# The prompt's second FFN product taken into the latents' seven products, and FFN stores issued by GpSimd

## The chip, the cores and the metric

The kernel runs on one core of a Trainium2 chip. The metric is the time of one execution in microseconds of the device; the kernel before was timed three times, with a median of 2180.29 us (2177.92 to 2182.85). The engines are TensorE (PE, matmuls), VectorE (DVE), ScalarE (ACT), GpSimd (POOL) and SyncE (SP); DMAs are issued from the instruction queues of SP, ACT or POOL and carried by 16 DMA engines.

## The reference, cut to what matters

One layer of a hybrid diffusion backbone on 1024 latent tokens and 256 prompt tokens, 1024 channels, all in float32. The token mixers come first and are not touched. What matters here is the end of the layer, which both kinds of token go through with the same weights, but with their own modulation (`sh2`, `sc2`, `g2`):

```python
    h = rms_norm(x, norm_ffn_w) * (1.0 + sc2) + sh2
    x = x + g2 * (jnp.square(jax.nn.relu(h @ w_ff1)) @ w_ff2)
...
y_prompt = rms_norm(xp, final_norm_w)
y_sample = rms_norm(xs, final_norm_w)
```

`w_ff1` is 1024 x 4096 and `w_ff2` 4096 x 1024. The other three outputs (keys, values and scan states of the prompt) are written long before.

## The kernel before, in words

**Splitting.** Every float32 product is made of three matmuls on two halves of each operand: `split` writes the high half on ACT (L270) and the rest on DVE (L271), and PE adds high x high, high x low and low x high (L299 to L301 in the first product, L1309 to L1311 and L1434 to L1436 in the latents' products, L1565 to L1567 in the prompt's second).

**The prompt's first product** (loop at L1255) goes over 16 blocks `i` of 256 of the 4096 hidden channels, each in two half-blocks of 128. A half-block loads its share of `w_ff1` (tile `wraw`, two buffers), splits it (`wsp`), and runs 24 matmuls of 128x256, the weights standing and the 256 prompt tokens moving. ACT takes relu and square into `ap` (L1232 to L1234, two buffers), and one store a block puts both halves into a DRAM tensor `AP_[i]`. Beside it, DVE and ACT prepare the latents' activations: their second norm, the sums that the seven products need (`sums1`, L1241 to L1251) and their splits (`form`).

**The latents' first product** (loop at L1313) computes, for each of the 16 blocks, a 2x2 block product in seven products instead of eight (Winograd's form of Strassen's scheme: sums of weight quarters against sums of activation quarters). Three PSUM banks X, Y, Z are used by turns: product 1 into X, which ACT copies to `s1` (L1318); product 2 into Y, to which DVE adds `s1` as `u2` (L1321); product 3 adds to X; and so on. Each block gives the four quarters after relu and square and the three sums that the second product needs. These seven forms go to DRAM with seven stores a block (L1348 to L1355), each of 512 columns, issued, as all stores of `store` (L101), from ACT's queue.

**The latents' second product** runs its seven products one after the other, in the order P1, P2, P6, P7, P4, P5, P3 (`chain2`, L1422). A product has 16 steps, one for each 256 hidden channels; a step loads one form of the activations (`ar`) and a weight quarter (`wr`, or `a11c` in P1, kept for later) three steps ahead, splits both (`ah`, `wh`) and runs 12 matmuls of 128x512 into four banks. Between the products DVE adds a product's banks to the residual (`gadd`, L1449, and the sums `u2`, `u3`). Within P5 the first half of the latents is normed and stored (`final`, L1459).

**The prompt's second product** follows as a stage of its own: 32 steps, each of which loads 128 rows of `w_ff2` again, splits them (`w2s`), and runs 12 matmuls of 128x512 with the prompt's activations standing (`mm_p`, L1559). The second half of the latents is normed beside it, and `final_p` (L1569) norms and stores the prompt at the end.

Each engine runs its instructions in the order of its own list, which a scheduler fixes when the kernel is built; an instruction that waits holds up all behind it on that engine. Tiles come from pools with a fixed number of buffers: a new tile in a used buffer waits for the old one's last readers, stores included. The pool `ev` of the latents' first product is opened where the pool `pw` of the prompt's was closed, so its tiles lie on the same memory.

Of the kernel before, what the change touches and what calls it, by code (L numbers as in the profile page):

```python
# [9 lines left out]
F32 = mybir.dt.float32  # L10
# [5 lines left out]
P = 128  # L16
D = 1024
# [27 lines left out]
def build(ctx, tc, I, O, C):  # L45
# [55 lines left out]
    def store(out, in_):  # L101
        s_.dma_start(out=f32(out), in_=f32(in_))
# [1125 lines left out]
    AP_ = [DR((P, 2, 256), "AP%d" % i) for i in range(NP)]  # L1228
    AF_ = {f: [DR((P, 512), "AF%s_%d" % (f, i)) for i in range(NP)] for f in FORMS}
# [26 lines left out]
    for i in range(NP):  # L1256
        r = raw1(i)
        for half in range(2):
# [5 lines left out]
            if half == 0:  # L1264
                e = pw.tile([P, 2, 256], F32, tag="ap", name="ap", bufs=2)
            relu2(e[:, half], po[:, 0:256])
            if half:
                store(AP_[i], e)
# [44 lines left out]
    for i in range(NP):  # L1313
# [34 lines left out]
        store(AF_["B11"][i], a11)  # L1348
        store(AF_["B22"][i], a22)
        store(AF_["T1"][i], t1)  # L1350
        store(AF_["T3"][i], t3)
        store(AF_["B21"][i], a21)
        store(AF_["T2"][i], t2)
        v.tensor_tensor(a12, a21, t2, op=ALU.subtract)
        store(AF_["T4"][i], a12)  # L1355
# [5 lines left out]
    sc2 = pool("s2c")  # L1361
    ac = pool("a11c", "right")
    a11c, s2c = {}, {}
# [14 lines left out]

    def load_a11(i):
        a11c[i] = quarter((0, 0), i, ac.tile([P, 512], F32, tag="a11_%d" % i, name="a11c"))  # L1380
        return a11c[i]

    def make_s2(i, x, y):
        s = wsum(x, y, ALU.add)
        s2c[i] = sc2.tile([P, 512], F32, tag="s2_%d" % i, name="s2c")
        v.tensor_tensor(s2c[i], s, a11c[i], op=ALU.subtract)
# [12 lines left out]
    def load_step(n):  # L1399
# [4 lines left out]
        ar = st.tile([P, 512], F32, tag="ar", name="ar", bufs=4)  # L1404
        dma(ar, AF_[STEP[name][0]][i])
# [8 lines left out]
        if n == 54:  # L1414
            load_fw()

    def rsp(tag, src):
        hi, lo = [st.tile([P, 512], F32R, tag=tag, name=tag, bufs=8) for _ in range(2)]
        split(hi, lo, src)
        return hi, lo  # L1420

    def chain2(name, banks, first, at=None):  # L1422
        for i in range(NP):
# [3 lines left out]
            ah, al = rsp("ah", ar)  # L1427
            wh, wl = rsp("wh", STEP[name][2](i, *ws_))
# [3 lines left out]
            for m in range(4):  # L1432
                c = slice(m * P, (m + 1) * P)
                pe.matmul(banks[m], wh[:, c], ah, start=first and i == 0, stop=False, **more)  # L1434
                pe.matmul(banks[m], wh[:, c], al, start=False, stop=False, **more)  # L1435
                pe.matmul(banks[m], wl[:, c], ah, start=False, stop=i == NP - 1, **more)  # L1436
# [7 lines left out]
    def cs(name):  # L1444
        return xo.tile([P, 512], F32, tag="cs", name=name, bufs=12)
# [14 lines left out]
    def final(t, b):  # L1460
# [3 lines left out]
        for i in range(2):  # L1464
# [3 lines left out]
            jk = xo.tile([P, 512], F32, tag="jk", name="jk", bufs=1)  # L1468
            s_.activation(jk, pt, AF.Square, accum_out=ss[:, i:i + 1])
# [3 lines left out]
        for i, pt in enumerate(pts):  # L1473
            y = xo.tile([P, 512], F32, tag="y", name="y", bufs=3)
# [3 lines left out]
    def four():  # L1478
        return [PS(x) for x in "ggss"]

    def load_p(kb):

        if kb >= NK:
            return
        early = kb < NQ1
        p, k = (q1, "e") if early else (q2, "l")
        if kb % 2 == 0 or kb == NQ1:
            aps[0] = p.tile([P, 2, 256], F32, tag="apr" + k, name="apr", bufs=2 if early else 4)
            dma(aps[0], AP_[kb // 2])
        wr = p.tile([P, D], F32, tag="w2p" + k, name="w2p", bufs=1 if early else 4)  # L1490
        dma(wr, W2[kb * P:(kb + 1) * P, :])
        got_p[kb] = aps[0][:, kb % 2], wr

    def prep_p(kb):
        early = kb < NQ1
        p, k = (q1, "e") if early else (q2, "l")
        ar, wr = got_p.pop(kb)
        hl = p.tile([P, 2, 256], F32R, tag="aph" + k, name="aph", bufs=NQ1 if early else 6)
# [154 lines left out]
```

## Time and profile before

| what | value |
|---|---|
| median of 3 runs | 2180.29 us |
| profiled execution | 2176.4 us, its span 2174.6 us, mean granted clock 0.988 |
| PE busy | 2085.2 us (96% of the span) |
| DVE, ACT, POOL busy | 1410.5, 981.1, 445.2 us |
| prompt's first product | 1341.0 to 1432.7 us |
| latents' first product | 1432.7 to 1742.3 us |
| latents' second product | 1749.9 to 2072.8 us |
| prompt's second product and last norms | 2072.8 to 2174.6 us |

Times in the trace are counted from the span's start. A row of a group gives the line, the engine, what it writes and reads with sizes, the count, busy time and mean, and the idle time of the engine just ahead of it with what ended it. A row of a timeline gives start, duration and, in brackets, idle time before. Rows with a q at the engine's name (ACTq, SPq) are the issue of a DMA in that engine's queue; POOL's own issues stand under POOL.

### The profile page before, as it was taken

The page shows a single profiled execution, that of the slowest core. Times are in us where ns is not written, and L with a number is a line of the kernel's source. Part 1 is how long each engine was busy: PE and PEld are TensorE (multiplying, and loading weights), DVE is VectorE, ACT ScalarE, POOL GpSimd, SP SyncE. Part 2 cuts the span into 40 slices and gives each one's busy share as a digit, 9 for nine tenths or more (in the row PEclk, how much of TensorE's full clock was granted, in tenths as well). Part 3 has the DMA queues.
Part 4 walks back from the last instruction along what each step waited for, and adds up shares of the span by engine and source line. Part 5 has one row for each costly group of instructions (what it writes and reads, how often), then busy time and mean ns, then how long its engine had stood idle before and what let it go on. Part 6 is the DMA issues. An engine that isn't in the chain of part 4 may idle for free. (4 is left out here: it accounts for less than half of the span.)

```text
span 2174.6 us, 34820 instructions
## 1 busy us (share of the span) xinstructions
PE 2085.2 (96%) x12907; PEld 1795.3 (83%) x12907; DVE 1410.5 (65%) x2642; ACT 981.1 (45%) x1994; POOL 445.2 (20%) x416
## 2 busy tenths in 40 slices
PE   6899999999999998999999999999999989999998
PEld 4788889988899877787888888988888878887786
DVE  3784776777776867768353536856666577666765
ACT  4754555555555422222220426745444444444453
POOL 1471233333233445445112000000000000000000
PEclk9999999999999999999999999999999999999999
DMA  9364222132122434445534433754444397567673
GB/s 287 106 201 141 69 73 70 53 117 78 53 68 74 148 117 147 142 144 160 191 127 131 128 117 107 225 173 138 157 137 154 134 318 264 188 196 254 220 273 138
DMA packets 266186, 327.14 MB, mean 150 GB/s; under 512 B 18952, under 2 KB 172112, under 8 KB 266016
## 3 DMA queue, kind: packets, MB, share of 16 engines
q1 hardware_dynamic: 244384, 285.80, 41.1%
q10 hardware_dynamic: 21312, 38.81, 4.8%
q8 instruction: 101, 1.65, 0.3%
q0 software_dynamic: 320, 0.31, 0.1%
q14 instruction: 69, 0.57, 0.1%
HBM read 240.44 MB, written 84.41 MB: 149 GB/s over the span
## 5 line engine op out<-in xcount | busy, mean ns | idle before, releaser
L299 PE MATMUL ps_g<-hs,wsp 128*128 128x512 f32 (+1 forms) x960 | 360.1, 375 | 2.4 <-DVE modc L190 2.4
L301 PE MATMUL ps_g<-hs,wsp 128*128 128x512 f32 (+1 forms) x960 | 343.6, 358 | 0.0
L300 PE MATMUL ps_g<-hs,wsp 128*128 128x512 f32 (+1 forms) x960 | 343.1, 357 | 0.0
L677 POOL TENSOR_SCALAR pexp<-pexp,rs 128x512 f32<-128x512 f32 (+1 forms) x104 | 169.1, 1632 | 367.7 <-ACT pTh L702 179.3
L270 ACT ACTIVATE wsp<-wraw 128x1024 fp32r<-128x1024 f32 x118 | 117.9, 1001 | 245.6 <-PE ps_g L300 115.1
L271 DVE TENSOR_TENSOR wsp<-wraw,wsp 128x1024 fp32r<-128x1024 f32 x118 | 141.9, 1204 | 121.0 <-ACT wsp L270 120.6
L299 PEld LDWEIGHTS ps_g<-hs,wsp 128*128 128x128 f32 x960 | 183.9, 192 | 27.2 <-issue 4.8
L301 PEld LDWEIGHTS ps_g<-hs,wsp 128*128 128x128 f32 x960 | 182.8, 190 | 27.5
L300 PEld LDWEIGHTS ps_g<-hs,wsp 128*128 128x128 f32 x960 | 183.9, 192 | 19.7
L702 ACT ACTIVATE pTh<-ps_t 128x512 fp32r<-128x512 f32 x200 | 119.0, 601 | 130.4 <-PE ps_t L699 127.4
L164 POOL TENSOR_TENSOR frst<-ms,mexp 128x1 f32<-128x1 f32 x10 | 7.2, 719 | 813.4 <-DVE ms L163 803.7
L659 DVE TENSOR_REDUCE mx<-ps_s 128x1 f32<-128x512 f32 (+1 forms) x208 | 136.7, 662 | 50.4 <-PE ps_s L658 49.8
L669 ACT ACTIVATE pexp<-ps_s,ngm 128x512 f32<-128x512 f32 (+1 forms) x208 | 137.3, 669 | 44.9 <-DVE ngm L663 43.3
L270 ACT ACTIVATE ah<-ar 128x512 fp32r<-128x512 f32 x112 | 70.7, 631 | 163.5 <-PE ps_s L1435 141.5
L703 DVE TENSOR_TENSOR pTl<-ps_t,pTh 128x512 fp32r<-128x512 f32 x200 | 135.8, 679 | 13.1 <-ACT pTh L702 12.7
L658 PE MATMUL ps_s<-Kl,Ql 128*128 128x512 f32 (+1 forms) x416 | 128.6, 413 | 1.5 <-ACT pexp L669 1.5
L699 PE MATMUL ps_t<-ident,pexp 128*128 128x128 f32 x800 | 120.7, 272 | 2.4 <-DVE pexp L677 1.3
L315 PE MATMUL ps_g<-wsp,hs 128*128 128x256 f32 x400 | 117.0, 292 | 0.0
L316 PE MATMUL ps_g<-wsp,hs 128*128 128x256 f32 x400 | 113.6, 284 | 2.8 <-DVE wsp L271 2.8
L317 PE MATMUL ps_g<-wsp,hs 128*128 128x256 f32 x400 | 113.6, 284 | 0.0
L271 DVE TENSOR_TENSOR ah<-ar,ah 128x512 fp32r<-128x512 f32 x112 | 77.1, 688 | 54.8 <-ACT ah L270 53.4
L715 PE MATMUL ps_g<-pTl,Vl 128*128 128x256 f32 x400 | 105.6, 286 | 4.5 <-DVE pTl L703 4.5
(362 smaller groups left out, 5449.8 us busy)
## 6 DMA issues: line engine op xcount, KB each, us to landing
wraw<-in_w_ff SPq DMA_DIRECT2D x32, 1024.0 KB, 5.7
wr<-in_w_ff SPq DMA_DIRECT2D x128, 256.0 KB, 4.0
wraw<-in_w_in SPq DMA_DIRECT2D x19, 1024.0 KB, 6.0
wraw<-in_w_ada SPq DMA_DIRECT2D x16, 1024.0 KB, 5.4
ar<-AFT SPq DMA_DIRECT2D x64, 256.0 KB, 2.7
w2p<-in_w_ff SPq DMA_DIRECT2D x32, 512.0 KB, 4.7
AFB<-a ACTq DMA_DIRECT2D x48, 256.0 KB, 2.2
AFT<-t ACTq DMA_DIRECT2D x48, 256.0 KB, 2.1
```

The lines of the kernel that those rows point to most:

```text
L270: s_.activation(hi, raw, AF.Copy)
L271: v.tensor_tensor(lo, raw, f32(hi), op=ALU.subtract)
L299: pe.matmul(out, hi[:, k, :], mh, start=(first and k == 0), stop=False)
L300: pe.matmul(out, hi[:, k, :], ml, start=False, stop=False)
L301: pe.matmul(out, lo[:, k, :], mh, start=False, stop=(last and k == kcs - 1))
L658: pe.matmul(pq[:, 0:n], self.qh[:, q0:q0 + P], K[self.g][var][self.kts[i]], start=(var == 0), stop=(var == 1))
L659: v.tensor_reduce(self.mx[j][:, i:i + 1], pq[:, 0:n], axis=AX.X, op=ALU.max)
L669: s_.activation(e[:, 0:n], self.ps.pop((j, i))[:, 0:n], AF.Exp, bias=self.mx[j], accum_out=self.sm[j][:, i:i + 1])
L677: NORM[(i + j) % len(NORM)].tensor_scalar(x, x, self.rs[j], None, op0=ALU.mult)
L699: pe.transpose(pt[:, a, j * P:(j + 1) * P], self.Ps[j][i][:, b * P:(b + 1) * P], ident)
L702: s_.activation(hi, pt, AF.Copy)
L703: v.tensor_tensor(lo, pt, f32(hi), op=ALU.subtract)
```

## The change

All stores of `store` are issued by GpSimd. The stores of the prompt's and the latents' activations now go to one DRAM tensor a block, `AFD[i]`, of seven forms by 640 columns: 512 of the latents, 128 of the prompt. For that, the prompt's 256 hidden channels of a block and its two halves of 128 tokens are taken as a 2x2 block matrix too, and DVE makes the four sums of its quarters as four subtractions of 128x128 into a tile `apf` with one buffer; three stores a block replace one.

In the second product a step loads 640 columns and splits them together; its weights, split for the latents, serve the prompt as well: three further matmuls of 128x512 (`mm_p`), into a fifth bank. P3's prompt matmuls are put off to the end: its split weights and activations are kept, in buffers that `a11c` and the sums `s2c` no longer need, and run there as 48 matmuls, alternating with the norms of the latents' second half. The stage of the prompt's second product goes, with its loads and splits. `final_p(0)` moves into P5. The output buffers `y` go from 3 to 2, the buffers `cs` for sums and copies of products from 12 to 8; they now also serve the squares' unused output and the prompt's sums.

```diff
     def store(out, in_):
-        s_.dma_start(out=f32(out), in_=f32(in_))
+        g_.dma_start(out=f32(out), in_=f32(in_))
...
-    AP_ = [DR((P, 2, 256), "AP%d" % i) for i in range(NP)]
-    AF_ = {f: [DR((P, 512), "AF%s_%d" % (f, i)) for i in range(NP)] for f in FORMS}
+    AFD = [DR((P, 7, 640), "AF%d" % i) for i in range(NP)]
...
             if half:
-                store(AP_[i], e)
+                f = pw.tile([P, 4, P], F32, tag="apf", name="apf", bufs=1)
+                b11, b12, b21, b22 = e[:, 0, 0], e[:, 0, 1], e[:, 1, 0], e[:, 1, 1]
+                v.tensor_tensor(f[:, 0], b12, b11, op=ALU.subtract)
+                v.tensor_tensor(f[:, 1], b22, b12, op=ALU.subtract)
+                v.tensor_tensor(f[:, 2], b22, f[:, 0], op=ALU.subtract)
+                v.tensor_tensor(f[:, 3], b21, f[:, 2], op=ALU.subtract)
+                store(AFD[i][:, 0:2, 512:640], e[:, :, 0])
+                store(AFD[i][:, 2, 512:640], b22)
+                store(AFD[i][:, 3:7, 512:640], f)
...
-        ar = st.tile([P, 512], F32, tag="ar", name="ar", bufs=4)
-        dma(ar, AF_[STEP[name][0]][i])
+        ar = st.tile([P, 640], F32, tag="ar", name="ar", bufs=4)
+        dma(ar, AFD[i][:, FI[STEP[name][0]]])
...
+    def mm_p(bank, i, a, w, first, last):
+
+        (ph, pl), (wh, wl) = a, w
+        more = dict(skip_group_check=not first)
+        pe.matmul(bank, ph, wh, start=first and i == 0, stop=False, **more)
+        pe.matmul(bank, pl, wh, start=False, stop=False, **more)
+        pe.matmul(bank, ph, wl, start=False, stop=i == NP - 1, **more)
...
+            if name != "P3":
+                mm_p(banks[4], i, (ah[:, 512:640], al[:, 512:640]), (wh, wl), first, False)
...
     def cs(name):
-        return xo.tile([P, 512], F32, tag="cs", name=name, bufs=12)
+        return xo.tile([P, 512], F32, tag="cs", name=name, bufs=8)
...
-            y = xo.tile([P, 512], F32, tag="y", name="y", bufs=3)
+            y = xo.tile([P, 512], F32, tag="y", name="y", bufs=2)
...
+    chain2("P2", X, False, {2: make_g2b})
...
+    chain2("P6", Y, True)
+    for m in range(4):
+        gadd(1, m, plus(Y[m], sk[m]))
+    padd(1, 0, plus(Y[4], sk[4]))
+    chain2("P7", Y, False)
...
+    at = {3 * b + 2: lambda b=b: final(0, b) for b in range(4)}
+    at[14] = lambda: final_p(0)
+    chain2("P5", Z, True, at)
+    for m in range(4):
+        gadd(1, 4 + m, Z[m])
+    padd(1, 1, Z[4])
+    chain2("P3", Z, False)
+    for m in range(4):
+        gadd(1, m, Z[m])
+    for i in range(NP):
+        mm_p(Z[4], i, p3f[i], p3w[i], False, True)
+        if i % 4 == 3:
+            final(1, i // 4)
+    padd(1, 0, Z[4])
+    final_p(1)
```

Three places show how the engines' lists change. In the rows, the names in brackets are what an instruction waits for: an engine, or a counter of landed DMAs (DMAHW for those that SP or ACT issued, DMASW for those of POOL).

First, DVE in the prompt's first product. In before, `wsp` are the low halves of the weights of half-blocks 18 and following (the first row is half-block 19), `form` and `xa` belong to the latents' sums:

```order
L271 TENSOR_TENSOR form<-xa,form 128x512 [waits DVE_49]
L1251 TENSOR_TENSOR xa<-xa 128x512 [waits DVE_49]
L271 TENSOR_TENSOR wsp<-wraw,wsp 128x1024 [waits PE_49,Activation_49]
L271 TENSOR_TENSOR form<-xa,form 128x512 [waits Activation_49]
L271 TENSOR_TENSOR wsp<-wraw,wsp 128x1024 [waits DMAHW0_49,PE_49,Activation_49]
L271 TENSOR_TENSOR form<-xa,form 128x512 [waits Activation_49]
L271 TENSOR_TENSOR wsp<-wraw,wsp 128x1024 [waits PE_49,Activation_49]
```

After the change, the same place on DVE; `apf` 4 is the first group of four, `apf` 5 the second:

```order
L1252 TENSOR_TENSOR xa<-xa 128x512 [waits DVE_49]
L271 TENSOR_TENSOR form<-xa,form 128x512 [waits Activation_49] x2
L1271 TENSOR_TENSOR apf<-ap 128x128 [waits DMASW7_49]
L1272 TENSOR_TENSOR apf<-ap 128x128
L1273 TENSOR_TENSOR apf<-ap,apf 128x128 [waits DVE_49]
L1274 TENSOR_TENSOR apf<-ap,apf 128x128 [waits DVE_49]
L1271 TENSOR_TENSOR apf<-ap 128x128 [waits DMASW2_49,DVE_49]
L1272 TENSOR_TENSOR apf<-ap 128x128
L271 TENSOR_TENSOR wsp<-wraw,wsp 128x1024 [waits PE_49,Activation_49]
L1273 TENSOR_TENSOR apf<-ap,apf 128x128 [waits DVE_49]
L1274 TENSOR_TENSOR apf<-ap,apf 128x128 [waits DVE_49]
L271 TENSOR_TENSOR wsp<-wraw,wsp 128x1024 [waits DMAHW0_49,PE_49,Activation_49]
```

Both last `form` rows now stand ahead of the weights of half-block 19, and so do `apf` 4 and, with its wait for the store of `apf` 4 (DMASW2), the first half of `apf` 5.

Second, the passage from the prompt's to the latents' first product. DVE before: the last split ahead of the latents' loop, and `u2` of the first block (`u`):

```order
L271 TENSOR_TENSOR wsp<-ws,wsp 128x1024 [waits PE_49,Activation_49]
L1292 TENSOR_TENSOR ws<-wraw,ws 128x512 [waits DVE_49]
L1321 TENSOR_TENSOR u_16765<-ps_s,s_16751 128x512 [waits PE_49,Activation_49]
L271 TENSOR_TENSOR wsp<-wraw,wsp 128x512 [waits PE_49,Activation_49]
L271 TENSOR_TENSOR wsp<-wraw,wsp 128x1024 [waits PE_49,Activation_49]
```

DVE after, from `apf` 13 on; the split and `apf` 12 stand just ahead of these rows:

```order
L1271 TENSOR_TENSOR apf<-ap 128x128 [waits DMASW2_49,DVE_49]
L1272 TENSOR_TENSOR apf<-ap 128x128
L1273 TENSOR_TENSOR apf<-ap,apf 128x128 [waits DVE_49]
L1274 TENSOR_TENSOR apf<-ap,apf 128x128 [waits DVE_49]
L1271 TENSOR_TENSOR apf<-ap 128x128 [waits DMASW5_49,DVE_49,Activation_49]
L1272 TENSOR_TENSOR apf<-ap 128x128 [waits Activation_49]
L1273 TENSOR_TENSOR apf<-ap,apf 128x128 [waits DVE_49]
L1274 TENSOR_TENSOR apf<-ap,apf 128x128 [waits DVE_49]
L1271 TENSOR_TENSOR apf<-ap 128x128 [waits DMASW0_49,DVE_49,Activation_49]
```

ACT after, at the same place; the last row is the copy `s1` of the first block, which before waited for PE alone:

```order
L270 ACTIVATE wsp<-ws 128x1024 [waits PE_49]
L1234 ACTIVATE ap<-ps_s 128x256 [waits DMASW6_49,DMASW5_49,DVE_49]
L1234 ACTIVATE ap<-ps_g 128x256
L1235 ACTIVATE ap<-ap 128x256 [waits Activation_49] x2
L1234 ACTIVATE ap<-ps_s 128x256 [waits DMASW1_49,DMASW0_49,DVE_49]
L1234 ACTIVATE ap<-ps_g 128x256 [waits PE_49]
L1235 ACTIVATE ap<-ap 128x256 [waits Activation_49] x2
L1327 ACTIVATE s_16751<-ps_g 128x512 [waits DMASW2_49,DMASW4_49,DMASW1_49,DMASW5_49,DMASW0_49,DMASW7_49,DVE_49,PE_49]
```

Four `apf` groups moved between the last split and `u2`, each behind the landing of the one before, and `s1` now waits for six counters, that of the last `apf` store (DMASW1) among them.

Third, ACT at the start of the latents' second product, before. The rows L102 are stores:

```order
L1234 ACTIVATE a_19030<-a_19030 128x512 [waits Activation_49]
L270 ACTIVATE ah<-ar 128x512 [waits DMAHW1_49]
L102 DMA AFT_15_15490<-t_19036 128x512 [waits DMAHW6_49,DVE_49]
L102 DMA AFB_15_15442<-a_19030 128x512 [waits DMAHW0_49,Activation_49]
L102 DMA AFT_15_15458<-t_19035 128x512 [waits DMAHW2_49,DVE_49]
L102 DMA AFT_15_15522<-u_18955 128x512 [waits DMAHW4_49,DVE_49]
L270 ACTIVATE wh<-a11c 128x512
```

And after:

```order
L1234 ACTIVATE a_19030<-a_19030 128x512 [waits DVE_49]
L1235 ACTIVATE a_19030<-a_19030 128x512 [waits Activation_49]
L270 ACTIVATE ah<-ar 128x640 [waits DMAHW6_49]
L270 ACTIVATE wh<-a11c 128x512 [waits DMAHW7_49]
L270 ACTIVATE ah<-ar 128x640 [waits DMAHW0_49]
```

The four stores ahead of the first split of weights are gone from ACT's list.

More of the change, by code (lines that the diff above doesn't have):

```diff
@@ L1556, in build, with five @@
[L1556 to L1567 removed]
+    def five():
+        return [PS(x) for x in "ggssg"]
```

211 lines of the change are left out of this document (80 added, 131 removed).

## The prediction

> **What bounds the kernel now.** I read first the busy times by stage, cut where the matmuls change line; the columns are the stretch, its length, then busy microseconds of PE, weight load, DVE, ACT and POOL, the granted clock, the DMA share and GB/s. In order: the prompt's first FFN product, the latents' first product, a gap, the latents' second product, the prompt's second product with the last norms.
>
> ```profile
> 1341.00:1432.70 91.70, 88.60 (x740) 87.25 (x739) 72.15 (x90) 71.56 (x130) 1.53 (x1) 1.00 0.69 217
> 1432.70:1742.30 309.60, 309.60 (x1346) 252.00 (x1344) 191.24 (x261) 146.22 (x222) 0.00 (x0) 1.00 0.42 142
> 1742.30:1749.90 7.60, 0.16 (x1) 0.00 (x0) 3.78 (x6) 2.42 (x5) 0.00 (x0) 0.69 0.76 261
> 1749.90:2072.80 322.90, 315.25 (x1376) 258.74 (x1377) 225.84 (x360) 139.10 (x248) 2.91 (x4) 0.98 0.72 240
> 2072.80:2165.30 92.50, 92.50 (x433) 77.02 (x431) 56.55 (x85) 46.54 (x80) 3.75 (x5) 1.00 0.62 213
> ```
>
> PE is busy in all of it, so matmuls left out pay in full and a stall on any engine that PE waits for costs in full. The waits of PE in the first of these stages name its only supplier that is late, the DVE half of the weight split:
>
> ```profile
> PE ps_g L301 <- DVE wsp L271: 1.8, 2, 1.1
> PE ps_s L301 <- DVE wsp L271: 1.3, 2, 0.9
> ```
>
> So that stage, which the change loads with DVE work, is already limited by DVE in places.
>
> **Gains, in the second product.** First the group of a product's matmuls by its two kinds of bank (total, mean ns, idle time before), then single matmuls (start, duration, idle time before in brackets).
>
> ```profile
> L1434 PE MATMUL ps_g<-ah,wh 128*128 128x512 f32 x224 | 89.0, 397 | 14.2 <-ACT wh L270 7.5 <-DVE xa L1449 6.7
> L1434 PE MATMUL ps_s<-ah,wh 128*128 128x512 f32 x224 | 88.5, 395 | 0.9 <-DVE u L1524 0.4 <-DVE xa L1449 0.3 <-DVE u L1529 0.2
> ```
>
> ```profile
> 2021.52 0.39 PE L1435 MATMUL ps_s<-ah,wh 128*128 128x512 f32 x1
> 2021.75 0.39 PE L1436 MATMUL ps_s<-ah,wh 128*128 128x512 f32 x1
> 2026.81 0.76 PE L1434 MATMUL ps_g<-ah,wh 128*128 128x512 f32 x1 [4.68 <-DVE xa L1449]
> ...
> 2032.01 0.39 PE L1434 MATMUL ps_g<-ah,wh 128*128 128x512 f32 x1
> ```
>
> A matmul of 512 columns follows the last by 0.227 us (2021.52 to 2021.75); after an idle 4.7 us, 12 of them take 2032.01 - 2026.81 = 5.2, 0.43 each: 5.2 - 12 x 0.227 = 2.4 us of lost clock for each long idle time.
> - Matmuls: the prompt's 384 become 7 x 48 = 336. 48 x 0.227 = **-10.9 us**. 288 run inside the steps (+65.4 us there), 48 at the end.
> - Start of the product: the next rows are ACT's queue and ACT.
>
> ```profile
> 1744.19 0.63 ACT L1234 ACTIVATE a<-a 128x512 f32<-128x512 f32 x1 [0.34 <-ACT a L1233]
> ...
> 1745.40 0.95 ACTq L102 DMA_DIRECT2D AFT<-t  x1
> 1748.88 0.33 ACTq L102 DMA_DIRECT2D AFT<-u  x1
> 1749.25 0.63 ACT L270 ACTIVATE wh<-a11c 128x512 fp32r<-128x512 f32 x1 [3.92 <-DMA AFT<-t]
> ```
>
> The first split of weights stood behind a store that waited for an earlier store. Without stores, ACT ends its last square at 1744.8, splits 640 and 512 columns (0.7 and 0.6), and PE starts near 1745.9 instead of 1749.9: **-4.0 us**.
> - Stalls between the seven products: 14.2 - 7.5 + 0.9 + 2.4 of clock = 10 us. A step lasts 15 x 0.227 = 3.40 us instead of 2.72 for 225.84/112 = 2.0 us of DVE, to which 128 more columns add some 0.13 us; this relief works for it, fewer shared buffers (12 to 8) that put DVE's sums of products between PE and its next weights work against it. I take **0** (bounds +5 and -10).
> - End: before, 101.8 us from the end of the last latent product (2072.8) to 2174.6, of which 384 x 0.227 = 87.1 matmuls: 14.7 of other work. After, the last 48 matmuls alternate with four norms, whose two PSUM banks and two output buffers free at the store's landing. One norm to its second output:
>
> ```profile
> 2162.76 0.17 DVE fss L1578
> 2163.82 0.76 DVE yo L1583
> 2164.61 2.12 DMA out_y_prompt<-yo
> ```
>
> ```profile
> L102 ACTq DMA_DIRECT2D out_y_prompt<-yo x4: 338/338/339, 2164.6 to 2171.5; - x4
> ```
>
> First 12 matmuls 2.7; transposes, squares and these steps about 4.5; three more norms at a period of about 3.9 (y at 2163.82, its store landed at 2166.73, then the next y) 11.7; the prompt's own last pair 3.6; last store to the end 2174.6 - 2171.5 = 3.1. Sum 25.6, of it 10.9 matmuls: 14.7, as before. The gate transposes that move into P2 add 1.8: **+1.8** (bounds 0 and +8).
> Sum: -10.9 - 4.0 + 0 + 1.8 = **-13.1 us** (bounds 0 and -25). W2 is no longer read twice and 32 splits go, but they ran under PE's 92.50: nothing. 64 stores become 160; POOL had no work in these stages.
>
> **Losses, in the first product.** Here the new work is `apf`: per block of 256 channels four DVE operations of 128x128 in one single buffer, whose store must have landed before the next block's first operation. This is the DVE queue around half-block 19 of 32 in before, and PE's start of it:
>
> ```profile
> 1393.98 1.21 DVE L271 TENSOR_TENSOR wsp<-wraw,wsp 128x1024 fp32r<-128x1024 f32 x1
> 1395.12 0.68 DVE L271 TENSOR_TENSOR form<-xa,form 128x512 fp32r<-128x512 f32 x1
> 1396.05 1.23 DVE L271 TENSOR_TENSOR wsp<-wraw,wsp 128x1024 fp32r<-128x1024 f32 x1 [0.25 <-ACT wsp L270]
> 1397.20 0.68 DVE L271 TENSOR_TENSOR form<-xa,form 128x512 fp32r<-128x512 f32 x1
> 1397.83 1.23 DVE L271 TENSOR_TENSOR wsp<-wraw,wsp 128x1024 fp32r<-128x1024 f32 x1
> 1403.42 2.36 DVE L271 TENSOR_TENSOR wsp<-wraw,wsp 128x1024 fp32r<-128x1024 f32 x2 [4.36 <-ACT wsp L270]
> ```
>
> ```profile
> 1396.06 0.28 PE L299 MATMUL ps_g<-h2p,wsp 128*128 128x256 f32 x1
> ```
>
> DVE has no gap up to 1399, and PE begins half 19 0.9 us after its weights (1393.98 + 1.2). In the new order these weights stand behind the two last form splits (2 x 0.6), `apf` 0 to 4 and two operations of `apf` 5, which wait for the store of `apf` 4. Prices, the first two of them a 128x128 operation and the landing of the old `AP` stores in this stage (min, median, max), then landings and POOL's issue elsewhere:
>
> ```profile
> L429 DVE TENSOR_TENSOR vst<-kve,vst 128x128 fp32r<-128x128 f32 x10 | 3.1, 335 | 0.9 <-ACT vst L428 0.9
> ```
>
> ```profile
> DMA to landing us min/median/max: 2.0/3.9/6.0
> ```
>
> ```profile
> AFT<-t ACTq DMA_DIRECT2D x48, 256.0 KB, 2.1
> mask<-const_masks POOLq DMA_DIRECT2D x2, 64.0 KB, 8.2
> rows<-in_b_ada POOLq DMA_DIRECT2D x1, 24.0 KB, 3.3
> ```
>
> ```profile
> 3.94 0.51 POOL L122 DMA_DIRECT2D rows<-in_hgrn_lb_logits  x1
> ```
>
> A 128x128 operation lasts 0.34 us there; 512 columns are followed after 0.63 (1397.20 to 1397.83), a quarter of which is 0.16. I take 0.25, in between, and 1.0 for the four. The turnaround t, from `apf`'s end to the next `apf`, is two semaphores (an estimate of 0.1 each), the landing, and POOL's issue, 0.2 us longer than ACT's 0.33. Bounds 2.1 (nearest store, quiet DMA) and 6.4 (AP's slowest), 8.2 for POOL's own at the program's start, when DMA was full. In this stage (DMA share 0.69) I take AP's 3.9 + 0.4 = 4.3; after it (0.42) between AFT's 2.1 + 0.4 and POOL's least 3.3 + 0.2: 3.1.
> - Half 19: 1.2 + 22 x 0.25 + 4.3 - 0.9 = **+10.1 us**, and **+2.4** of clock. From there a block's DVE loop is 1.0 + 4.3 = 5.3 us, two weight splits (2.3) lying in the wait, under PE's pitch of 91.7/16 = 5.7: no further loss unless t exceeds 4.7. Behind `apf` on ACT wait the squares of the block after next and with them its next splits; that loop is 4.8 us (1.4 squares, 1.0 split on ACT, 1.2 on DVE, 1.0 `apf`, 0.2), also covered. On POOL the next block's other two stores stand ahead of an `apf` store, issued by then.
> - The stage's end. Rows of ACT, then DVE:
>
> ```profile
> 1432.82 1.06 ACT L270 ACTIVATE wsp<-ws 128x1024 fp32r<-128x1024 f32 x1 [1.03 <-PE ps_g L300]
> 1433.79 0.36 ACT L1233 ACTIVATE ap<-ps_g 128x256 f32<-128x256 f32 x1
> 1435.73 0.60 ACT L1318 ACTIVATE s<-ps_g 128x512 f32<-128x512 f32 x1 [1.13 <-PE ps_g L1311]
> ```
>
> ```profile
> 1434.05 1.22 DVE L271 TENSOR_TENSOR wsp<-ws,wsp 128x1024 fp32r<-128x1024 f32 x1
> 1438.59 0.69 DVE L1321 TENSOR_TENSOR u<-ps_s,s 128x512 f32<-128x512 f32 x1 [2.72 <-PE ps_s L1311]
> ```
>
> PE leaves the stage at 1432.7 (call it 0). The split at 1434.05 waits for that end, so it is done at 2.4; in the new order `apf` 12, 13, 14 and 15 all stand behind it, each waiting for the one before to land. `apf` 12 with one sum: to 3.9. Then three times t + 1.0, then t until `apf` 15 has landed. Only then may the copy `s1` (L1318 before, 0.6) be written, since its tile lies where `apf` lay, and PE's third product of the latents, which adds to the bank that `s1` copies, stands behind it on PE. It was due at 24 x 0.23 = 5.5. Stall: 3.9 + 3.0 + 4t + 0.6 - 5.5 = 2.0 + 4t, at t = 3.1 **+14.4 us** (10.4 at 2.1, 27 at 6.4), and **+2.4** of clock. Nothing later gives it back: PE is busy 309.60 of the next 309.60.
> Sum of losses 10.1 + 14.4 + 4.8 = **+29.3 us**.
>
> The Trainium skill, page "SBUF — State Buffer", section "SBUF: two separate sides", speaks against stores on GpSimd: their descriptors are written by GpSimd, and a DVE copy in a two-port mode locks it out, so that a transfer of about 0.62 us took 3.1. No row here shows GpSimd issuing beside a busy DVE. By that rule each of the five turnarounds would be an estimated 2.5 us longer, and the sum 12 us higher.
>
> **Total.** -13.1 + 29.3 = +16.2 us on the profiled execution's 2176.4 (span 2174.6 and 1.8 around it): 2192.6. That execution lies 3.9 under the median 2180.3, so against the median the time is **2196.5**.
>
> **Rivals.**
> - The turnaround sets the stage's pace. If t is 6.4 in both places (AP's slowest), half 19 costs 12.2, six more blocks 6 x (7.4 - 5.7) = 10, the end 27.6, clock 4.8: +54.6 - 13.1, 2222. At t = 5: 10.8 + 2 + 22 + 4.8 - 13.1 = +26.5, 2207. For it: AP's range and POOL's 8.2; against: AP's median. By the Trainium skill's page it would be this case, 2209. Chance 0.22.
> - Half 19 isn't late: DVE has hidden room (shorter 128x128 operations, an early landing). Then 12.5 go and 2184 remains. Against: PE waited for DVE there already. Chance 0.12.
> - Not slower: the second product gains its full bound. With 3.40 us steps DVE is never late at the product boundaries (-10) and PE's start stays warm (-2.4): -25.5. It decides if all five boundaries show under 1 us of idle time. At my t that is 2184; with t = 2.6 in both places (losses 8.4 + 12.4 + 4.8) 2180.4, no change. Against: L1449's sums in DVE's queue remain. Chance 0.13.
>
> **How the numbers follow.** The forecast, both stalls paid and t near my values, has 0.53: 2187 to 2206. The range that leaves out 2 in 10 goes from 2179 (the third rival) to 2214 (t near 5.5). A run tells 0.2%, 4.4 us, from no change. Slower: forecast, first rival, a third of the second and third: 0.83. Within: most of those two, 0.12. Faster needs both bounds at once: 0.05.
>
> **What would show it.** Right: PE idle near 10 us in the prompt's first product with DVE `apf` behind a landing of its store, and 10 to 20 us after the latents' second product with ACT's `s1` behind that landing; the start of the second product idle under 4 us; under 30 us from P3's end. Wrong: PE without a gap there, `apf` to landing far from 3 to 4 us, or boundaries of the second product that cost over 15 us.

## The result, and the profile after

The changed kernel takes **2202.46 us** (median of 4 runs, 2200.76 to 2210.59) against 2180.65 for the kernel before on the same chip (4 runs, 2177.92 to 2182.85): a ratio of 1.0108, 95% interval 1.0081 to 1.0135, so slower by 0.8 to 1.35%. The prediction was 2196.5, with a range of 2179 to 2214.

The profiled execution is the longest of the four, 2210.59 (span 2208.5). Of the 34 us that lie between it and the profiled execution of before, 10.8 stand ahead of the prompt's first product, where nothing was changed (that product starts at 1346.3 in place of 1335.5). This is spread between runs: the median less the length of the stages from there on is 1340.3 for the changed kernel and 1341.6 for the kernel before. So stages are compared. The prompt's first product and the second product count from their own first matmul, the other stages from the end of the last matmul ahead of them. First the changed kernel; the columns are the stretch, its length, busy microseconds of PE, weight load, DVE, ACT and POOL, the granted clock, the DMA share and GB/s:

```profile
1346.30:1453.40 107.10, 96.35 (x785) 94.98 (x784) 84.90 (x141) 72.00 (x129) 25.88 (x38) 0.95 0.66 198
1453.40:1783.80 330.40, 312.71 (x1346) 253.87 (x1344) 198.46 (x282) 149.94 (x233) 65.26 (x118) 0.97 0.42 140
1783.80:1787.20 3.40, 0.15 (x2) 0.02 (x1) 3.13 (x6) 2.47 (x5) 1.59 (x3) 0.90 1.00 367
1787.20:2179.90 392.70, 385.19 (x1680) 314.83 (x1681) 250.34 (x390) 152.38 (x265) 10.30 (x18) 0.98 0.65 210
2179.90:2208.50 28.60, 15.93 (x81) 11.99 (x80) 10.71 (x24) 6.64 (x20) 8.38 (x15) 0.84 0.24 92
```

Then the first stage of the kernel before, from its first matmul, 5.5 us earlier than the prediction cut it:

```profile
1335.50:1432.70 97.20, 94.10 (x786) 92.71 (x785) 77.65 (x98) 77.06 (x139) 1.53 (x1) 1.00 0.65 206
```

| stage, us | before | after | difference | predicted |
|---|---|---|---|---|
| prompt's first product | 97.2 | 107.1 | +9.9 | +12.5 |
| latents' first product, with the passage into it | 309.6 | 330.4 | +20.8 | +16.8 |
| start of the second product | 7.6 | 3.4 | -4.2 | -4.0 |
| second product | 322.9 | 392.7 | +69.8 | +67.2 |
| after the last latent matmul | 101.8 | 28.6 | -73.2 | -76.2 |
| sum | 839.1 | 862.2 | +23.1 | +16.2 |

In the two first products PE was busy for the whole stretch or nearly so before; now it is idle 10.8 us (107.1 - 96.35) in the one, against 3.1 before, and 17.7 (330.4 - 312.71) in the other, against none. The waits of PE from the first product to the end say for what (engine, tile and line that waited; what it waited for; microseconds in total, times, the longest):

```profile
PE ps_g L1318 <- ACT s L1327: 15.4, 1, 15.4
PE ps_s L299 <- ACT ap L1234: 9.4, 2, 8.4
...
PE ps_s L1468 <- DVE u L1550: 2.9, 1, 2.9
PE ps_g L1468 <- DVE xa L1485: 2.6, 2, 2.4
PE ps_g L1318 <- ACT ap L1234: 2.3, 1, 2.3
```

**The passage.** This is the predicted chain, in the DVE queue behind the end of the prompt's first product (1453.4): a group of four operations on `apf`, and then 3.1 us of nothing until its store has landed.

```profile
1459.10 0.29 DVE L1271 TENSOR_TENSOR apf<-ap 128x128 f32<-128x128 f32 x1
...
1460.43 0.29 DVE L1274 TENSOR_TENSOR apf<-ap,apf 128x128 f32<-128x128 f32 x1
1463.84 0.29 DVE L1271 TENSOR_TENSOR apf<-ap 128x128 f32<-128x128 f32 x1 [3.12 <-DMA AF<-apf]
...
1468.00 0.29 DVE L1271 TENSOR_TENSOR apf<-ap 128x128 f32<-128x128 f32 x1 [3.13 <-DMA AF<-apf]
...
1472.16 0.29 DVE L1271 TENSOR_TENSOR apf<-ap 128x128 f32<-128x128 f32 x1 [3.14 <-DMA AF<-apf]
...
1472.89 0.29 DVE L1274 TENSOR_TENSOR apf<-ap,apf 128x128 f32<-128x128 f32 x1
```

The period is 4.16 us (1463.84 to 1468.00). ACT's copy `s1` comes 3.2 us after the last group has ended, when its store has landed, and PE goes on behind it. ACT's row, then PE's:

```profile
1476.41 0.60 ACT L1327 ACTIVATE s<-ps_g 128x512 f32<-128x512 f32 x1 [10.24 <-issue]
```

```profile
1477.06 0.79 PE L1318 MATMUL ps_g<-form,wsp 128*128 128x512 f32 x1 [15.36 <-ACT s L1327]
1477.65 0.63 PE L1319 MATMUL ps_g<-form,wsp 128*128 128x512 f32 x1
1478.08 0.63 PE L1320 MATMUL ps_g<-form,wsp 128*128 128x512 f32 x1
```

ACT's row names no releaser ("issue"), but the view of the tile `apf` lists who waited for it (us, times):

```profile
who waited for it (us, times):
...
  ACT ap L1234: 15.6, 11
  ACT s L1327: 10.2, 1
```

The matmuls behind the stall follow each other at 0.43 us (1477.65 to 1478.08) in place of 0.227: the lost clock of the prediction.

**The stall in the prompt's first product** is there too, but it came by another way than predicted. The group of the fourth block (`apf` 3) waits here for no store. Its four operations are spread over 8 us of DVE's own queue, between the forms of the latents' activations and the weight splits:

```profile
1397.44 0.30 DVE L1271 TENSOR_TENSOR apf<-ap 128x128 f32<-128x128 f32 x1
1397.64 0.30 DVE L1272 TENSOR_TENSOR apf<-ap 128x128 f32<-128x128 f32 x1
...
1399.65 1.24 DVE L271 TENSOR_TENSOR wsp<-wraw,wsp 128x1024 fp32r<-128x1024 f32 x1
1400.78 0.30 DVE L1273 TENSOR_TENSOR apf<-ap,apf 128x128 f32<-128x128 f32 x1
...
1404.52 0.71 DVE L271 TENSOR_TENSOR form<-t,form 128x512 fp32r<-128x512 f32 x1
1405.12 0.31 DVE L1274 TENSOR_TENSOR apf<-ap,apf 128x128 f32<-128x128 f32 x1
```

The last of them is the last reader of an `ap` buffer, of which there are two. ACT's next relu wants that buffer, and it is this relu that empties a PSUM bank for PE. The row of ACT, then those of PE ahead of the stall and behind it:

```profile
1405.46 0.38 ACT L1234 ACTIVATE ap<-ps_s 128x256 f32<-128x256 f32 x1 [0.17 <-DVE apf L1274]
```

```profile
1397.02 0.28 PE L299 MATMUL ps_g<-h2p,wsp 128*128 128x256 f32 x1
1397.14 0.28 PE L300 MATMUL ps_g<-h2p,wsp 128*128 128x256 f32 x1
...
1405.90 0.58 PE L299 MATMUL ps_s<-h2p,wsp 128*128 128x256 f32 x1 [8.36 <-ACT ap L1234]
1406.28 0.41 PE L300 MATMUL ps_s<-h2p,wsp 128*128 128x256 f32 x1
1406.49 0.41 PE L301 MATMUL ps_s<-h2p,wsp 128*128 128x256 f32 x1
```

So a full queue on DVE, not a landing, held PE (and the clock with it: matmuls at 0.21 us in place of 0.12). The chain of landings begins behind it, from 1408 on.

### The profile page after: what moved, and what is told of

Same layout as the page of the kernel before. It is cut to its first block, busy times and chain, and to the rows that moved or that the text cites. A ratio compares the mean times of both kernels' runs of the same rounds, so it can differ in the third digit from the quotient of the medians.

```text
span 2208.5 us, 34669 instructions
## 1 busy us (share of the span) xinstructions
PE 2089.4 (95%) x12859; PEld 1793.7 (81%) x12859; DVE 1398.2 (63%) x2666; ACT 951.6 (43%) x1947; POOL 548.5 (25%) x596
## 5 line engine op out<-in xcount | busy, mean ns | idle before, releaser
L270 ACT ACTIVATE ah<-ar 128x640 fp32r<-128x640 f32 (+1 forms) x112 | 81.1, 724 | 211.6 <-PE ps_g L1441 192.6
L271 DVE TENSOR_TENSOR ah<-ar,ah 128x640 fp32r<-128x640 f32 (+1 forms) x112 | 90.0, 804 | 81.3 <-ACT ah L270 81.1
L714 PE MATMUL ps_g<-pTh,Vl 128*128 128x256 f32 x400 | 105.5, 284 | 0.2 <-DVE ze L810 0.2
```

The lines of the kernel that those rows point to most:

```text
L270: s_.activation(hi, raw, AF.Copy)
L271: v.tensor_tensor(lo, raw, f32(hi), op=ALU.subtract)
```

## The experiments

All stages below are counted as in the table above; runs of one group were on one chip, beside the kernel before.

| kernel | time, us | ratio to before (95%) | prompt's first | latents' first | start | second | tail | sum |
|---|---|---|---|---|---|---|---|---|
| ring3 | 2187.16 | 1.0027 (1.0015 to 1.0040) | 98.8 | 323.2 | 3.4 | 389.5 | 28.5 | 843.4 |
| apf_elsewhere | 2195.83 | 1.0060 (1.0040 to 1.0080) | 107.6 | 325.1 | 3.4 | 389.3 | 28.5 | 854.0 |
| stores_on_act | 2196.05 | 1.0069 (1.0048 to 1.0090) | 111.2 | 323.4 | 4.9 | 387.1 | 25.6 | 852.3 |
| before_pool_stores | 2181.40 | 1.0004 (0.9992 to 1.0015) | 98.0 | 309.5 | 3.3 | 322.7 | 104.9 | 838.5 |
| apf_on_pool | 2204.39 | 1.0113 (1.0087 to 1.0139) | 109.0 | 330.4 | 3.4 | 391.8 | 28.5 | 863.1 |
| ring3_on_pool | 2195.53 | 1.0066 (1.0046 to 1.0086) | 107.2 | 324.5 | 3.4 | 389.3 | 28.6 | 853.0 |
| ring3_on_pool_out_act | 2193.85 | 1.0063 (1.0041 to 1.0085) | 105.5 | 326.0 | 3.4 | 387.0 | 26.4 | 848.3 |
| late_sums | 2174.51 | 0.9968 (0.9954 to 0.9982) | 100.4 | 309.6 | 3.4 | 389.2 | 28.9 | 831.5 |
| late_sums_out_act | 2176.20 | 0.9962 (0.9947 to 0.9976) | 100.9 | 309.6 | 3.4 | 392.3 | 25.7 | 831.9 |

The kernel before took 2181.39 in the first group of four, 2180.11 beside the next three, and 2183.49 beside the last two.

### Three buffers in place of one: ring3

The chain of landings needs a single buffer. Here `apf` shares a ring of three with `t1` and `t3`, in the same memory.

```diff
-                f = pw.tile([P, 4, P], F32, tag="apf", name="apf", bufs=1)
+                f = pw.tile([P, 512], F32, tag="t1", name="apf", bufs=3).rearrange("p (t c) -> p t c", t=4)
...
-            t1 = t1s[kb] = pw.tile([P, 512], F32, tag="t1", name="t1", bufs=2)
+            t1 = t1s[kb] = pw.tile([P, 512], F32, tag="t1", name="t1", bufs=3)
...
-            t3 = pw.tile([P, 512], F32, tag="t1", name="t3", bufs=2)
+            t3 = pw.tile([P, 512], F32, tag="t1", name="t3", bufs=3)
```

> The changed kernel, with apf in the ring of the tile t1, raised from two to three buffers, instead of a single buffer of its own. Theory (the chain apf, store, landing, next apf in one buffer, and s1 on its memory, make the loss): PE's stall ahead of the latents' third product falls from 15.4 us to under 2 and the stage of the prompt's first product from 107.0 to 100-103 (DVE's 64 subtractions, some 13 us of its queue, stay); time 2175 to 2183, about the kernel before. Rival (stores from GpSimd, or DVE's added work alone, make the loss): the time stays above 2195.

It took 2187.16, above the expected 2175 to 2183. The prompt's first product is nearly back (98.8), but the passage still costs 13.6 us, and the stall for `s1` is 4.8 us where under 2 was expected. The waits of PE in the two stages:

```profile
PE ps_g L1318 <- ACT s L1327: 4.8, 1, 4.8
PE ps_s L1319 <- DVE form L271: 3.6, 1, 3.6
...
PE ps_g L1320 <- DVE wsp L271: 1.7, 1, 1.7
```

No group waits for the landing of the group before any more, and still PE waits 10.1 us in the passage in three pieces. Two of them (5.3 us) are for DVE's ordinary work, which stands behind the sums in its queue. The ring itself holds this work up: `t1` and `t3` now take turns with `apf`, and DVE waits with them four times for the landing of an `apf` store (us, times):

```profile
  DMA AF<-apf: 6.1, 4
```

So the last of the latents' forms is split 111 us after the stage's first matmul, and 62 us after it in the changed kernel. The third piece (4.8 us) is `s1`, again behind a store of `apf`, in ACT's row:

```profile
1456.70 0.60 ACT L1327 ACTIVATE s<-ps_g 128x512 f32<-128x512 f32 x1 [5.97 <-DMA AF<-apf]
```

So taking the single buffer away gains 18.8 us by the stages (862.2 - 843.4; 17.7 by the two ratios). What is left of the loss is the sums' place on DVE, the waits that the ring brings and the memory of `s1`; this kernel doesn't part them.

### The buffer where nothing of the next stage lies on it: apf_elsewhere

```diff
-                f = pw.tile([P, 4, P], F32, tag="apf", name="apf", bufs=1)
+                f = ws.tile([P, 4, P], F32, tag="apf", name="apf", bufs=1)
```

> The changed kernel, with apf still in one buffer, but in a pool that stays open over the latents' first product, so that s1 lies on other memory. Theory: the chain of four landings at the stage's end stays, and with it u2 on DVE behind the last apf; only s1's wait for the last landing goes. PE's stall at the latents' third product falls to under 3 us, and a stall of 6 to 9 us for u2 comes two products later: time 2192 to 2197. Rival (the overlap of s1 with apf alone is the cause at that place): no stall for u2, time 2183 to 2188.

The time came as expected (2195.83), but not by the expected way: the stall at `s1` was to fall under 3 us, and one of 6 to 9 us for `u2` was to come. No stall for `u2` came, and the one at `s1` went from 15.4 to 12.3 only. `s1` no longer waits for `apf`'s last store, but for the end of the last group itself. The addresses of the tiles in the two built kernels say why: where `apf` lay, there now lies the last `ap` buffer, which the last group reads, and `s1` lies on that. The waits of PE, and ACT's row:

```profile
PE ps_g L1318 <- ACT s L1327: 12.3, 1, 12.3
PE ps_s L299 <- ACT ap L1234: 9.2, 2, 8.1
```

```profile
1467.00 0.60 ACT L1327 ACTIVATE s<-ps_g 128x512 f32<-128x512 f32 x1 [7.15 <-DVE apf L1274]
```

So where `apf` lies is worth about one landing (3.1 us). The chain ahead of it costs the rest, and the stall at the fourth block doesn't depend on where the buffer lies. A kernel with the chain and with `s1` on memory of its own was not run.

### The stores' queue: stores_on_act and before_pool_stores

The first takes back one line of the change, the second makes that line the only change to the kernel before.

```diff
     def store(out, in_):
-        g_.dma_start(out=f32(out), in_=f32(in_))
+        s_.dma_start(out=f32(out), in_=f32(in_))
```

> The changed kernel with all stores of the FFN and the outputs issued by ACT again. Theory: the chain stays and only a turnaround shrinks, from some 4.2 us to 3.4 (ACT's issue 0.33 instead of 0.75, landing 2.1 instead of 3.3): stage and passage gain 4 to 6 us, the start of the second product loses 4: 2198 to 2205. Rival (issuing from GpSimd is the cause): the loss goes, under 2185.

```diff
     def store(out, in_):
-        s_.dma_start(out=f32(out), in_=f32(in_))
+        g_.dma_start(out=f32(out), in_=f32(in_))
```

> The kernel before, with only the stores of the FFN and the outputs issued by GpSimd. Theory: the start of the latents' second product comes 4 us earlier, nothing else waits for these stores: 2174 to 2178 against 2180.6 before. Rival (stores from GpSimd cost by themselves): over 2183.

stores_on_act took 2196.05, a little under the expected 2198 to 2205: a landing is shorter from ACT's queue, so the chain is too (the stall at `s1` is 11.4), and the start of the second product loses 1.5 us where 4 were expected. But the first product is longer (111.2): PE waits there 5.7 us for DVE's splits of weights, in place of 1.4; why is not shown. The rows of the DMAs that store `apf`, of the changed kernel and then of stores_on_act (queue, count, size, median us from issue to landing):

```profile
AF<-apf POOLq DMA_DIRECT2D x16, 256.0 KB, 3.3
```

```profile
AF<-apf ACTq DMA_DIRECT2D x16, 256.0 KB, 2.6
```

before_pool_stores shows both sides of the line: the start of the second product gains 4.3 us, as predicted for the changed kernel, and the tail loses 3.1 (104.9 for 101.8), which neither the prediction nor this expectation had. Its time is that of before, above the expected 2174 to 2178. Most of the loss is behind the last store of the output: from its issue to the span's end it takes 5.3 us (2167.2 to 2172.5), and 3.1 in before (2171.5 to 2174.6). In the changed kernel POOL issues these stores too; the rows of the output tile at its end:

```profile
L102 POOL DMA_DIRECT2D out_y_prompt<-y x2: 540/560/579, 2202.7 to 2203.5; - x2
...
DMA to landing us min/median/max: 2.3/2.4/2.6
```

The last issue is at 2203.5 and the span ends at 2208.5, 5.0 us later. In stores_on_act the tail is 25.6, to the tenth what the prediction had summed up from ACT's landings.

### The sums on GpSimd: apf_on_pool, ring3_on_pool, ring3_on_pool_out_act

If DVE's queue is the trouble, the idle GpSimd might take the sums: with the single buffer, with the ring of three, and with the ring and the outputs stored by ACT.

```diff
-                v.tensor_tensor(f[:, 0], b12, b11, op=ALU.subtract)
-                v.tensor_tensor(f[:, 1], b22, b12, op=ALU.subtract)
-                v.tensor_tensor(f[:, 2], b22, f[:, 0], op=ALU.subtract)
-                v.tensor_tensor(f[:, 3], b21, f[:, 2], op=ALU.subtract)
+                g_.tensor_tensor(f[:, 0], b12, b11, op=ALU.subtract)
+                g_.tensor_tensor(f[:, 1], b22, b12, op=ALU.subtract)
+                g_.tensor_tensor(f[:, 2], b22, f[:, 0], op=ALU.subtract)
+                g_.tensor_tensor(f[:, 3], b21, f[:, 2], op=ALU.subtract)
```

> The changed kernel, with the four subtractions of apf on GpSimd instead of DVE; the single buffer and s1's wait for its last landing stay. Theory (what hurts is that DVE, in order, stands in front of weights and u2 while apf waits for a landing): the stage of the prompt's first product falls from 107 to 97.5-100 us, and s1 waits for one landing behind the last block: a stall of 2 to 5 us instead of 15.4 there; time 2178 to 2184. Rival (the chain of landings itself is the bound, on whichever engine: 4 operations of 0.66 us, 0.75 of issue and 2.6 of landing are 6 us a block against PE's 5.7): it runs behind PE by the stage's end and the passage stalls 8 us or more, time over 2188.

> The ring of three with the subtractions on GpSimd. Theory (what was left of the loss with the ring of three, 4.4 us over before from the stage's start on, is DVE's added 64 operations and the order they force on it: 1.6 us and 13.6 us in the two first products): first product 97 to 98.5, passage stall under 4 us, time 2168 to 2175. Rival (stores from GpSimd and the wait of s1 hold it): time 2183 or more.

> As the run before, with the output stores alone issued by ACT again. Theory (the tail of 28.6 us is 3 us longer with stores from GpSimd, as 25.6 with all stores on ACT shows): tail 25.3 to 26, time 2 to 3.5 us under that of the run before. Rival: the tail is set by the norms' own chain, no difference.

The first two expectations failed by about 20 us, and the times of their rivals came. With the single buffer the kernel is as slow with the sums on GpSimd as on DVE (863.1 for 862.2): the next group waits for the landing on whichever engine. With the ring the first product is 8.4 us longer than with the sums on DVE, and PE waits there 9.2 us for DVE's splits of weights in place of 4.2. Both engines are slower. First DVE's split of the weights in that stage, in ring3 and in ring3_on_pool (count, busy us, mean ns):

```profile
L271 DVE TENSOR_TENSOR wsp<-wraw,wsp 128x1024 fp32r<-128x1024 f32 x31 | 37.7, 1220 | 6.2 <-ACT wsp L270 6.0
```

```profile
L271 DVE TENSOR_TENSOR wsp<-wraw,wsp 128x1024 fp32r<-128x1024 f32 x30 | 41.4, 1383 | 17.4 <-ACT wsp L270 16.4 <-PE ps_g L301 0.9 <-PE ps_s L300 0.2
```

Then the sums themselves on GpSimd in ring3_on_pool (ns min, median, max):

```profile
L1271 POOL TENSOR_TENSOR apf<-ap x16: 449/898/1526, 1352.9 to 1457.6; 128x128 f32<-128x128 f32 x16
```

A sum takes 0.28 to 0.31 us on DVE; on GpSimd 0.45 at best and 0.90 in the median, while DVE's own splits grow by 13%. It is the two together that are slow: the sums that run while DVE is idle take 0.44 to 0.48 us, and one split of DVE's, from 1430.22 on, takes 3.15 us in place of 1.22 while four sums of 0.45 us run on GpSimd. This agrees with the Trainium skill, page "SBUF — State Buffer", section "SBUF: two separate sides": a DVE operation with two inputs in SBUF and a GpSimd operation that reads SBUF lock each other out. Storing the outputs from ACT brought the tail from 28.6 to 26.4, where 25.3 to 26 were expected; by the times the two kernels can't be told apart (1.0066 and 1.0063).

### The sums later: late_sums and late_sums_out_act

The last pair leaves the sums on DVE, but in the stage where it has room: busy 191.24 of 309.60 us in the kernel before. The prompt's first product stores its activation raw; the latents' first product loads one block in each of its 16 rounds of 19 us, sums and stores it.

```diff
+    AE = [DR((P, 2, 2, P), "AE%d" % i) for i in range(NP)]
...
-                f = pw.tile([P, 4, P], F32, tag="apf", name="apf", bufs=1)
...
+                store(AE[i], e)
                 store(AFD[i][:, 0:2, 512:640], e[:, :, 0])
-                store(AFD[i][:, 2, 512:640], b22)
-                store(AFD[i][:, 3:7, 512:640], f)
+                store(AFD[i][:, 2, 512:640], e[:, 1, 1])
...
-        return ev.tile([P, 512], F32, tag="ev", name=name, bufs=14)
+        return ev.tile([P, 512], F32, tag="ev", name=name, bufs=16)
...
+        e = E("ap").rearrange("p (h t c) -> p h t c", h=2, t=2)
+        dma(e, AE[i])
...
+        f = E("apf").rearrange("p (n c) -> p n c", n=4)
...
+        store(AFD[i][:, 3:7, 512:640], f)
```

> The four sums of a block leave the prompt's first product: there the activation is stored raw (one more store of 256 KB per block), and in the latents' first product, where DVE is busy 62% of the time, it is loaded back, summed and stored, one block per 19 us. Theory A: everything that the change lost in the first product and the passage came from where the sums stand. Then PE's stretch of the prompt's first product is 97 to 99 us (107.0 after, 97.2 before), the latents' first product 309.5 to 313 (330.4 after), the rest as after, together 828 to 834 against 839 before and 862 after: 2168 to 2175 us. Rival B: a good part of the loss is the stores' (160 in place of 64, all issued by GpSimd, and the raw one on top) or DVE's load wherever it stands: the latents' first product stays above 318, the total above 837, and the time at 2179 to 2190.

For late_sums_out_act the output rows are stored by ACT besides:

```diff
-            store(out_rows(t, b)[:, i * 512:(i + 1) * 512], y)
+            s_.dma_start(out=out_rows(t, b)[:, i * 512:(i + 1) * 512], in_=y)
...
-            store(out_rows(2, b)[:, c], y)
+            s_.dma_start(out=out_rows(2, b)[:, c], in_=y)
```

> As late_sums, with the output rows stored from ACT's queue again (all other stores stay on GpSimd's). Theory: the tail's period of a norm holds the landing of an output store, which is shorter from ACT's queue: tail 25.5 to 26.6 us in place of 28.5, second product 387 to 389 in place of 389.3, so 2 to 5 us under late_sums: 2164 to 2172 us. Rival: the tail's period is set by DVE's and ACT's own work and the queue doesn't matter: within 1.5 us of late_sums.

late_sums takes 2174.51 us and is the fastest kernel of the study together with its variant: 0.32% under the kernel before (0.18 to 0.46%), and 1.4% (some 30 us) under the changed one by the two ratios. Its stages, cut as at the start:

```profile
1345.10:1445.50 100.40, 95.19 (x786) 93.34 (x785) 76.54 (x97) 76.53 (x139) 28.61 (x46) 1.00 0.70 217
1445.50:1755.10 309.60, 309.60 (x1346) 251.80 (x1344) 206.95 (x322) 149.31 (x222) 70.74 (x125) 1.00 0.54 174
```

PE is busy for all 309.60 us of the latents' first product again, though DVE does 64 operations more there (206.95 us busy for 191.24) and GpSimd stores all the while. The passage costs nothing: rival B, by which the stores or DVE's load would cost a good part of the loss wherever they stand, falls. The first product is 3.2 us over before and 1.4 longer than expected (100.4 for at most 99): PE waits there 4.6 us for DVE's splits, 1.5 more than the four waits that before shows. This kernel takes away the sums' place, their single buffer and the memory under `s1` at once, so it shows what the three cost together, not each.

late_sums_out_act took 2176.20, above the expected 2164 to 2172: the tail is 25.7, as expected, but the second product was 3.1 us longer in its profiled execution, and by the times the two kernels can't be told apart (0.9962 and 0.9968, with overlapping intervals). That the 3 us of the tail are gained in the time isn't shown.

## Why the prediction was right, and where its terms were off

The case that had the highest chance came: both stalls are paid, and t in the passage is the value chosen. All stages together the loss is 23.1 us where 16.2 were predicted, and each stage is within 4 us of its term.

- **Half 19**, predicted +12.5, measured +9.9: the size was nearly right, but PE lost it by another route, so that the size fits is luck. The prediction let PE wait for weights behind `apf` 4 and 5 and one landing. In the trace PE waits three half-blocks earlier, at half 16, for a PSUM bank behind ACT's relu, which waits for an `ap` buffer that the sums free late. The step that failed is the sentence on the loop through ACT ("Behind `apf` on ACT wait the squares of the block after next", "that loop is 4.8 us"): it priced the loop with an empty queue on DVE, and there the sums of one group were 8 us apart. ring3 and late_sums show the stage at 98.8 and 100.4 once the single buffer, or the sums, are gone. That the stall in apf_elsewhere is the same (8.1) fits both routes. The predicted wait is there as well, on DVE, ahead of `apf` 5 and the weights of half 19:

```profile
1412.62 0.29 DVE L1271 TENSOR_TENSOR apf<-ap 128x128 f32<-128x128 f32 x1 [3.13 <-DMA AF<-apf]
...
1413.03 1.22 DVE L271 TENSOR_TENSOR wsp<-wraw,wsp 128x1024 fp32r<-128x1024 f32 x1
```

  These weights are ready at 1414.3. At the pace of before, where half 19 starts 60.5 us after the stage's first matmul, PE would have wanted them at 1406.8, an estimated 7.4 us earlier; but it had lost 8.4 us at half 16 and came at 1416.8. Behind that, the reckoning that nothing more is lost held: three turnarounds of the stage took 5.0 to 7.7 us, over the bound of 4.7, and PE didn't wait. Its pitch of 5.7 us fits by luck: the 91.7 us hold 15 blocks, not 16, which makes 6.1 on the mean, and the last six blocks of before take 5.6 each (1398.87 to 1432.7).
- **The passage**, predicted 2.0 + 4t with t = 3.1, and 2.4 of clock; measured +20.8 for 16.8. t is right to a few hundredths: DVE idles 3.12 to 3.14 a turn, and the last landing takes 3.2 to `s1`. What was undersized is the start: the group ahead of the three landings ended at 1460.7, 7.3 us after the stage's end, where 3.9 was reckoned, since the weight sums of the next block stood ahead of it, and PE lost 2.3 us to the relu of the last blocks before that. 17.7 us idle were 14.4 by the formula; the clock took the other 3.1, for 2.4.
- **The mechanism** is borne out by three kernels: a landing less in the wait for `s1` (apf_elsewhere), no chain (ring3, 7.2 us less in this stage), no sums (late_sums: +0.0 in this stage). Of the 10.1 us of waiting that ring3 leaves in the passage, 4.8 are for a landing under `s1` and 5.3 for DVE's work of the stage itself. What the place of the sums costs alone is not shown.
- **The Trainium skill's rule on descriptors** (page "SBUF — State Buffer", section "SBUF: two separate sides"), by which each turnaround would be an estimated 2.5 us longer, was not put to the test. It speaks of DVE copies in a two-port mode, and DVE ran no copy in these two stages. Beside its operations of two inputs POOL's issue of an `apf` store takes 0.75 to 0.76 us, as beside an idle DVE, and the landing 3.3 us in the median (ACT's queue: 2.6). In the chain of the passage DVE is idle during each turnaround.

Stores of the changed kernel by GpSimd in the two first products (issue in ns, min, median, max):

```profile
L102 POOL DMA_DIRECT2D AF<-apf x16: 750/750/760, 1361.1 to 1473.5; - x16
```

- **Start of the second product**, predicted -4.0, measured -4.2; before_pool_stores shows it alone (-4.3).
- **Stalls between the products**, predicted 0: idle time of PE in the second product is 7.5 us (392.7 - 385.19) for 7.7 before. The stage is 2.6 us over its term; its busy time grew by 69.9 for 65.4 of matmuls. The nine kernels that have this stage take 387.0 to 392.7 for it, 389.8 on the mean, which is 66.9 over before: the term was right, and the 2.6 lie within the spread. The rival that gains 10 us here (boundaries without idle time) is out: one boundary still costs 2.9 and one 2.4.
- **The end**, predicted 25.6 us of tail, measured 28.6. The period of a norm is as reckoned, 3.97 us for 3.9, by the two rows of DVE below. The term took the landing and the end from rows of ACT's queue, though the change had moved those stores to GpSimd's, whose price the same prediction had put higher for `apf`. 1.9 of the 3.0 us lie behind the last issue (5.0 for 3.1). stores_on_act has 25.6, late_sums 28.9 and late_sums_out_act 25.7.

```profile
2185.78 1.41 DVE L1510 SCALAR_TENSOR_TENSOR y<-ps_t,frst,fwb 128x512 f32<-128x512 f32 x2 [0.74 <-POOL frst L164]
...
2189.75 1.41 DVE L1510 SCALAR_TENSOR_TENSOR y<-ps_t,frst,fwb 128x512 f32<-128x512 f32 x2 [0.75 <-POOL frst L164]
```

- **Matmuls**: 48 fewer, reckoned at 10.9 us. The two last stages together gain 3.4 us in the changed kernel (421.3 for 424.7) and 6.6 in late_sums (418.1). With the start's 4.2, and less 3.2 in the first product, that makes the change a gain of 7.6 us by the stages of late_sums, 7 by its ratio, once the sums stand where DVE has room.

## What to carry to other kernels

A tile with one buffer makes its producer wait for the landing of its own store, and on an engine that runs in order all of that engine's later work waits too: price the chain at the place where the producer's queue has caught up, mostly at the end of a stage, and look at what the next stage's memory lies on. Ask for each added operation not only how long it takes but in which stage its engine has room: the same 64 small sums cost some 30 us more, through a single buffer, in one stage than through a ring of buffers in the next. And when a change moves transfers to another queue, take every price from that queue, down to the last store of the program.

## What the runs showed of the hardware

- A store of 256 KB in four pieces a row lands 3.3 us (median; 2.7 to 7.3) after its issue by GpSimd and 2.6 by ACT in the same stages, and the issue itself holds GpSimd 0.75 us and ACT 0.37; one of a single piece holds GpSimd 0.54 to 0.58, and ACT 0.33 to 0.34. Behind the last store of the program the span goes on for 5.0 to 5.3 us with GpSimd and 3.1 to 3.2 with ACT.
- After an idle time of 8.4 us the matmuls of 256 columns came at 0.21 us in place of 0.12, after 15.4 us those of 512 at 0.43 in place of 0.227; after 2.3 us (1455.85) these came at 0.23. The whole stage of the first has 2.3 us more of busy PE than before (96.35 for 94.10).
- Two-input operations on GpSimd and DVE slow each other: from 0.45 us alone to 0.90 in the median on GpSimd for 128x128, and from 1.22 to 1.38 in the mean on DVE for 128x1024.
